# A recurrent layer whose convolution stays in fp32, with its products on VectorE and its squares on ScalarE

## The chip, the core and the metric

The kernel runs on one core of one Trainium2 chip. The time is the device time of one execution in microseconds (us), before: 1421.28 us, the median of three runs (1419.26 to 1422.52). The engines are TensorE (PE in the profile; its weight loads are PEld), VectorE (DVE), ScalarE (ACT), GpSimd (POOL) and the queue SyncE (SP), which issues most of the loads.

## The reference

A trunk of two layers over 512 tokens of 1024 features. Each layer is a mixer, a cross-attention into 256 memory tokens and a SwiGLU FFN, each with a norm in front and a residual add behind. Layer 1's mixer is the recurrent block on which the change works:

```
z = h @ w_in                                   # [512, 2048]
gate_branch, xb = split(z, 2)
xb = causal_depthwise_conv(xb, conv_w, conv_b) # width 4
r = sigmoid(xg @ w_rgate + b_r); i = sigmoid(xg @ w_igate + b_i)   # 4 heads of 256
log_a = -8 * r * softplus(-lam)
a = exp(log_a); mult = sqrt(-expm1(2 * log_a)) # a = 0 and mult = 1 where positions == 0
b = mult * (i * xb)
hseq = scan: h[t] = a[t] * h[t-1] + b[t]
y = (gelu(gate_branch) * hseq) @ w_out
```

The cross-attention of a layer norms the memory, with a gain of that layer, and makes keys and values of it: `m = rms_norm(mem, norm_mem[layer]); k, v = split(m @ w_kv, 2)`.

## The kernel before

Activations lie with features on the partitions, as tiles of 128 features by 512 tokens. Every product of TensorE is made of three: weights and activations are each split into a high part (float32r) and a low part (what is left), and `mm3` sums high by high, high by low and low by high (lines 166, 167 and 168). One output tile of 128 features from 1024 is 24 matmuls of 512 columns.

**Weights.** `Weights.get` loads 512 KB over SP into one of two raw buffers (tag `wraw`), casts it on ScalarE to the high part (line 98) and subtracts on VectorE for the low part (line 99); there are three buffers for each part. So VectorE has one subtraction of 1024 columns for each output tile.

**Banks.** `linear` writes to a PSUM bank with the tag `mm` or `att`; there are two of each. A third tile on `mm` needs the first one read out.

**The recurrent block (`odd`).** `conv_tile(m)` makes one tile of xb, multiplies it by the norm's row (826), runs the four taps on VectorE (829, 831) into a temporary `t0`, and splits that into high and low for the gate products (153, 154). `lru_gates` makes the tiles `r` and `i` of a head (sigmoids, 841); then GpSimd adds the high and low part of the convolution to get it back (879) and multiplies `i` by it (880), VectorE scales `r` (881), and ScalarE writes tanh into a tile `h` (841). `gate_tile(m)` makes a tile of the gate branch and VectorE reads it out of `mm` (904, tile `g`). `lru_scan` runs exp on all eight `r`, squares them on GpSimd (890, into `t0`, of which there are two), combines on VectorE (891), runs sqrt on ScalarE, multiplies (895) and scans (896) on VectorE. ScalarE needs one table for exp, another for sqrt and another for GeLU, and `run()` keeps each kind together. Then GpSimd multiplies GeLU of the gate by the scan (918), the result is split (153, 154) and goes into `out_proj`.

**The memory.** `mem_gained(layer, ...)` loads the memory, multiplies it by its norm's row on GpSimd (348) and splits it with the layer's gain on ScalarE and VectorE (156, 157) into the tile `mg`. `odd` calls it for layer 1 and makes the keys (`mem_keys`, weights `xk`, copies out of `mm` at 362); `cross(1)` calls it once more for the values.

**Order.** A scheduler works out the order of each engine from a timeline of its own when the program is built. What it may move it moves, over the borders of the stages too. `tc.issue_after` holds some instructions behind others.

Of the kernel before, what the change touches and what calls it, by code (L numbers as in the profile page):

```python
# [9 lines left out]
F32 = mybir.dt.float32  # L10
# [3 lines left out]
AF = mybir.ActivationFunctionType  # L14
ALU = mybir.AluOpType
AX = mybir.AxisListType
PSUM = bass.MemoryType.PSUM

P = 128
T = 512  # L20
D = 1024
KD = D // P
# [46 lines left out]
class Weights:  # L69
    """Streams [n, 128, F] blocks and splits each into float32r high and low parts."""  # L70
# [33 lines left out]
class Trunk:  # L104
# [23 lines left out]
    def pair(self, side, n=T):  # L128
        """High and low parts of an activation tile, from one of the two sides of the activation store."""
        return tuple(self.actp.tile([P, n], F32R, name=self.nm(f"act{side}"), tag=f"act{side}") for _ in range(2))  # L130
# [7 lines left out]
    def bank(self, tag="mm"):  # L138
        """A PSUM bank: mm and att for products, s for scores, tr for transposes and row sums."""
        if tag == "any":  # L140
            self.flip ^= 1
            tag = ("mm", "att")[self.flip]
        return self.psum.tile([P, T], F32, name=self.nm(tag), tag=tag, bufs=BANKS[tag])
# [15 lines left out]
    def mm3(self, out, terms, begin=True, end=True):  # L159
        """out = sum over terms of (wh + wl).T @ (xh + xl), less wl.T @ xl.  # L160

        A sum in pieces has its first one with begin and its last one with end."""
        nc = self.nc
        last = len(terms) - 1
        for i, (wh, wl, xh, xl) in enumerate(terms):
            nc.tensor.matmul(out, wh, xh, start=begin and i == 0, stop=False)  # L166
            nc.tensor.matmul(out, wh, xl, start=False, stop=False)  # L167
            self.mm_ins = nc.tensor.matmul(out, wl, xh, start=False, stop=end and i == last).ins  # L168

    def rstd_cols(self, *sums, inner=None, bank="tr"):  # L170
        """For each (ssq, dim, tiles, scale): [128, tiles] columns of scale * rsqrt(column sums of ssq / dim + eps).

        With inner the squared values are still to be scaled by these columns, and so is what the result scales."""
        nc = self.nc
        ps = self.bank(bank)
        n = sum(s[2] for s in sums)
        v = self.small(8)
        o = 0
        for ssq, dim, nt, _ in sums:
            terms = ssq if isinstance(ssq, tuple) else (ssq,)  # L180
            for t in range(nt):
                for i, a in enumerate(terms):
                    self.sum_ins = nc.tensor.matmul(ps[:, o + t:o + t + 1], a[:, t * P:(t + 1) * P], self.ones[:, 0:1],  # L183
                                                    start=i == 0, stop=i == len(terms) - 1).ins
            o += nt
        o = 0
        if inner is not None:
            sq = self.small(8)
            nc.vector.tensor_mul(sq[:, :inner.shape[-1]], inner, inner)
        for _, dim, nt, _ in sums:  # L190
            if inner is None:
                nc.vector.tensor_scalar(v[:, o:o + nt], ps[:, o:o + nt], 1.0 / dim, EPS, op0=ALU.mult, op1=ALU.add)
            else:
                nc.vector.scalar_tensor_tensor(v[:, o:o + nt], ps[:, o:o + nt], 1.0 / dim, sq[:, :nt],
                                               op0=ALU.mult, op1=ALU.mult)
            o += nt
        if inner is not None:
            nc.vector.tensor_scalar(v[:, :n], v[:, :n], EPS, None, op0=ALU.add)
        r = self.rsqrt(v, n)
        res, o = [], 0  # L200
        for _, _, nt, scale in sums:
            if inner is not None:
                nc.vector.scalar_tensor_tensor(r[:, o:o + nt], r[:, o:o + nt], scale or 1.0, inner,
                                               op0=ALU.mult, op1=ALU.mult)
            elif scale is not None:
                nc.vector.tensor_scalar(r[:, o:o + nt], r[:, o:o + nt], scale, None, op0=ALU.mult)
            res.append(r[:, o:o + nt])
            o += nt
        return res

    def rsqrt(self, v, n):
        """v ** -0.5 of n columns, refined by one step."""
        nc = self.nc
        y, w, r = (self.small(8)[:, :n] for _ in range(3))
        v = v[:, :n]
        nc.gpsimd.tensor_tensor(y, v, self.mhalf[:, :n], op=ALU.pow)
        nc.vector.tensor_mul(w, y, y)
        nc.vector.tensor_mul(w, w, v)
        nc.vector.tensor_scalar(w, w, -0.5, 1.5, op0=ALU.mult, op1=ALU.add)
        nc.vector.tensor_mul(r, y, w)  # L220
        return r

    def bcast(self, cols, nt=NT, bank="tr"):
        """PSUM tile [128, nt*128] with the columns' values along the free axis, on every partition."""
# [27 lines left out]
    def next_norm(self, side, gain, off):  # L252
        """State for the norm that follows a residual update: filled tile by tile."""
        return {"side": side, "gain": gain, "off": off, "ssq": self.new_ssq(), "xg": []}
# [9 lines left out]
    def linear(self, W, blk, xs, off=0, bank="mm", ps=None, k0=0, k1=None):  # L264
        """One output tile: block blk of W holds its k tiles side by side. With k0 and k1 a piece of the sum."""
# [18 lines left out]
    def setup(self):  # L284
# [6 lines left out]
        # the table of the first functions is loaded before there is data  # L291
        nc.scalar.activation(self.small(1), self.ones[:, 0:1], AF.Square)
        # the array's clock is raised while the first operands are on their way
# [29 lines left out]
    def mem_load(self, keys):  # L323
        """The memory, feature tiles of [128, 256], in the place of the keys to come or among the inputs."""
# [9 lines left out]
    def mem_gained(self, layer, pool, tag, keys=True):  # L334
        """The memory's norm with the layer's gain, split: feature tiles [128, 256], high and low."""
# [17 lines left out]
    def mem_keys(self, layer, mg, m0, m1, low=None):  # L353
        """Keys of the memory, [features, memory tokens]."""
# [9 lines left out]
    def rope_table(self, pool, C):  # L364
        """C: rows 0:64 one, 64:96 cos, 96:128 sin with the sign of its half.

        Worked out with 16 frequencies x 8 chunks of the positions on the partitions."""
# [49 lines left out]
    def even(self, nrm, nxt_spec):  # L417
# [4 lines left out]
        with ExitStack() as ctx:  # L422
# [10 lines left out]
            # latents: z[0:2] of the queries, z[2] of keys and values, z[3] rotary keys and their swapped halves  # L433
# [36 lines left out]
            # queries and keys of two pairs of heads; rows 64:128 of the keys stay  # L470
# [10 lines left out]
            # pooling mixer  # L481
# [31 lines left out]
            # latent attention  # L513
# [22 lines left out]
            def v_pair(wh, wl):  # L536
                """Values of two heads, tokens on partitions."""
# [99 lines left out]
    def cross(self, layer, nrm, nxt_spec, mg=None):  # L637
# [3 lines left out]
        with ExitStack() as ctx:  # L641
# [40 lines left out]
            def scores(hd):  # L682
                """Softmax of one head's scores, queries on partitions, two query tiles side by side."""
# [63 lines left out]
    def ffn(self, layer, nrm, nxt_spec):  # L747
# [12 lines left out]
        for pi, nf in enumerate(FFN_PARTS):  # L760
# [3 lines left out]
            for f in range(f0, f0 + nf):  # L764
                pg = self.linear(Wg, (layer * NF + f) * 2, xg, bank="mm")
                pu = self.linear(Wg, (layer * NF + f) * 2 + 1, xg, bank="att")
                if R is None:
                    R = self.norm_row(nrm["ssq"], D)
                t = self.tmp("t0")
# [17 lines left out]
    def odd(self, nrm, nxt_spec):  # L787
# [6 lines left out]
        with ExitStack() as ctx:  # L794
# [6 lines left out]
            # 8 * softplus(-lambda) = 8 * (max(-lambda, 0) + log1p(exp(-|lambda|)))  # L801
# [20 lines left out]
            def conv_tile(m, bank="mm"):  # L822
# [4 lines left out]
                t = self.tmp("t0")  # L827
# [11 lines left out]
            def act(out, src, fn, **kw):  # L839
                """A function of ScalarE's tables; run() keeps those of a kind together."""  # L840
                table.append(nc.scalar.activation(out, src, fn, **kw).ins)
# [12 lines left out]
            def lru_gates():  # L854
                for hd in range(4):
                    if hd == 0:
                        # the row of the norm's factors comes between the first tiles
# [10 lines left out]
                    for d in range(2):  # L868
# [8 lines left out]
                        xh, xl = xc[m]  # L877
                        x = self.tmp("t1")
                        nc.gpsimd.tensor_add(x, xh[:, :].bitcast(F32), xl[:, :].bitcast(F32))
                        nc.gpsimd.tensor_mul(is_[m], is_[m], x)  # L880
                        nc.vector.scalar_tensor_tensor(rs[m], rs[m], c8[:, m:m + 1], rst, op0=ALU.mult, op1=ALU.add)
                        ts[m] = pool.tile([P, T], F32, name=f"h{m}", tag=f"h{m}")
                        act(ts[m], rs[m], AF.Tanh)

            def lru_scan():
                with run():
                    for m in ms:
                        a2 = self.tmp("t0")
                        act(rs[m], rs[m], AF.Exp, scale=-1.0)
                        nc.gpsimd.tensor_mul(a2, rs[m], rs[m])  # L890
# [19 lines left out]
            mg = self.mem_gained(1, pool, "mg")  # L910
            gates = [gate_tile(m) for m in range(KD)]
            self.mem_keys(1, mg, 0, KD, None)
# [4 lines left out]
            for m, t in enumerate(gates):  # L917
                nc.gpsimd.tensor_mul(hs[m], t, hs[m])
# [7 lines left out]
    def tail(self, W, ys, base, side):  # L926
        """The last projection, its residual and the final norm: features on partitions for the first tokens,
        tokens on partitions for the last ones."""
# [38 lines left out]
        def after(n):  # L967
            """The sums and the row of the norm come in between these products."""
# [31 lines left out]
def tile_trunk(ctx: ExitStack, tc: tile.TileContext, ins, out):  # L1000
    k = Trunk(ctx, tc, ins, out)
    nrm = k.setup()
    stages = [
        lambda n: k.even(n, ("xa_norm_x", 0)),
        lambda n: k.cross(0, n, ("ffn_norm", 0)),
        lambda n: k.ffn(0, n, ("od_norm", 0)),
        lambda n: k.odd(n, ("xa_norm_x", KD)),
        lambda n: k.cross(1, n, ("ffn_norm", KD)),
        lambda n: k.ffn(1, n, None),
    ]  # L1010
    for s in stages:
        nrm = s(nrm)
# [78 lines left out]
```

## Time and profile before

| | |
|---|---|
| span of the profiled execution | 1418.8 us |
| its own time | the profile gives the span alone |
| median of the runs | 1421.28 us (1419.26 to 1422.52) |
| instructions | 16758 |
| busy PE, DVE, ACT, POOL | 1384.2, 784.9, 549.6, 321.7 us |
| mean granted TensorE clock | 0.989 of full speed |
| the recurrent block | about 710 to 912 us of the span |

Busy times are sums of instructions of an engine over the span. Where a matmul follows another, the profile counts TensorE as busy throughout, so a share near 100% is the most that can be read there. A wait is named after the engine whose work ended it.

### The profile page before, as it was taken

How to read it: one execution, taken by the hardware profiler on the slowest of the kernel's cores; microseconds unless marked ns; L12 is line 12 of the kernel's file. 1: busy time of each engine (PE TensorE's matmuls, PEld its weight loads, DVE VectorE, ACT ScalarE, POOL GpSimd, SP SyncE). 2: the span in 40 equal slices, each digit the busy share in tenths (PEclk: the TensorE clock that was granted, in tenths of full speed). 3: DMA queues.
4: the chain of work that ended last, by engine and by line, in shares of the span. 5: the costliest groups of instructions: out<-in, count | busy, mean ns of one | idle time of the engine just before them, and what ended most of it. 6: DMA issues, size and time to landing. Idle time of an engine off the chain costs nothing.

```text
span 1418.8 us, 16758 instructions
## 1 busy us (share of the span) xinstructions
PE 1384.2 (98%) x6524; PEld 1153.3 (81%) x6524; DVE 784.9 (55%) x1043; ACT 549.6 (39%) x859; POOL 321.7 (23%) x291
## 2 busy tenths in 40 slices
PE   8989999999999999999999989999999999999997
PEld 6878888878888888888887778888888888888887
DVE  7687574456454345344579796445545534453553
ACT  6466553454332232223434555335433312221331
POOL 4586261103110011001234470211121100110112
PEclk8999999999999999999999989999999999999999
DMA  6222162323223233332322334322323333323331
GB/s 208 75 71 79 60 193 79 115 60 118 90 90 104 89 104 92 102 90 93 108 89 90 98 105 154 96 71 91 116 89 93 100 96 98 99 84 111 93 104 60
DMA packets 45326, 140.28 MB, mean 99 GB/s; under 512 B 5568, under 2 KB 10816, under 8 KB 45248
## 3 DMA queue, kind: packets, MB, share of 16 engines
q1 hardware_dynamic: 43808, 137.91, 31.1%
q10 hardware_dynamic: 1440, 1.32, 0.3%
q8 instruction: 51, 0.84, 0.2%
q14 instruction: 27, 0.22, 0.0%
HBM read 136.98 MB, written 2.10 MB: 98 GB/s over the span
## 4 chain that ended last, share of the span: by engine, by line
PE 86%; DVE 7%; issue 2%; ACT 2%; DMA 1%; POOL 1%; POOLq 0%; SPq 0%; ACTq 0%; DVEq 0%
PE mm L166 16%; PE mm L168 16%; PE mm L167 16%; PE att L166 10%; PE att L168 10%; PE att L167 10%; DMA dn_raw<-in_ffn_down_dram 1%; DVE h L896 1%; DVE act L154 1%; PE s L166 1%; PE s L167 1%; PE s L168 1%; DVE i L895 1%; PE tr L183 1%; PE mm L667 1%
## 5 line engine op out<-in xcount | busy, mean ns | idle before, releaser
L98 ACT CAST gu_h<-gu_raw 128x1024 fp32r<-128x1024 f32 x88 | 92.8, 1054 | 293.0 <-PE mm L167 162.7
L774 POOL TENSOR_TENSOR t<-t,t 128x512 f32<-128x512 f32 x44 | 60.0, 1364 | 577.9 <-ACT gu_h L98 383.1
L99 DVE TENSOR_TENSOR gu_l<-gu_raw,gu_h 128x1024 fp32r<-128x1024 f32 x88 | 138.2, 1570 | 33.1 <-ACT gu_h L98 33.1
L166 PE MATMUL att<-act,gu_h 128*128 128x512 f32 x352 | 137.8, 391 | 0.0
L166 PE MATMUL mm<-act,gu_h 128*128 128x512 f32 x352 | 137.1, 390 | 0.0
L168 PE MATMUL att<-act,gu_l 128*128 128x512 f32 x352 | 137.0, 389 | 0.0
L167 PE MATMUL mm<-act,gu_h 128*128 128x512 f32 x352 | 136.9, 389 | 0.0
L168 PE MATMUL mm<-act,gu_l 128*128 128x512 f32 x352 | 136.9, 389 | 0.0
L167 PE MATMUL att<-act,gu_h 128*128 128x512 f32 x352 | 136.9, 389 | 0.0
L247 POOL TENSOR_TENSOR ssq<-ssq,t 128x512 f32<-128x512 f32 (+1 forms) x49 | 77.5, 1582 | 196.5 <-ACT t L246 188.5
L773 DVE TENSOR_TENSOR t<-att,R 128x512 f32<-128x512 f32 x44 | 30.4, 691 | 128.3 <-PE att L168 128.3
L98 ACT CAST dn_h<-dn_raw 128x1024 fp32r<-128x1024 f32 (+1 forms) x40 | 40.3, 1011 | 138.2 <-PE att L167 102.5
L167 PEld LDWEIGHTS att<-act,gu_h 128*128 128x128 f32 x352 | 66.2, 188 | 14.2 <-issue 0.5
L166 PEld LDWEIGHTS att<-act,gu_h 128*128 128x128 f32 x352 | 66.0, 188 | 14.1 <-issue 0.5
L168 PEld LDWEIGHTS mm<-act,gu_l 128*128 128x128 f32 x352 | 66.1, 188 | 13.9
L168 PEld LDWEIGHTS att<-act,gu_l 128*128 128x128 f32 x352 | 66.0, 188 | 13.7
L167 PEld LDWEIGHTS mm<-act,gu_h 128*128 128x128 f32 x352 | 66.0, 187 | 13.7
L166 PEld LDWEIGHTS mm<-act,gu_h 128*128 128x128 f32 x352 | 66.1, 188 | 13.5
L274 DVE TENSOR_TENSOR x<-mm,x 128x512 f32<-128x512 f32 x44 | 30.3, 690 | 83.4 <-PE mm L168 82.6
L770 DVE TENSOR_TENSOR t<-mm,R 128x512 f32<-128x512 f32 x44 | 30.4, 691 | 69.6 <-PE mm L168 66.8
L153 ACT CAST act<-t 128x512 fp32r<-128x512 f32 (+1 forms) x53 | 32.9, 621 | 71.9 <-POOL t L774 56.0
L99 DVE TENSOR_TENSOR dn_l<-dn_raw,dn_h 128x1024 fp32r<-128x1024 f32 (+1 forms) x40 | 56.2, 1408 | 6.6 <-ACT dn_h L98 6.6
(397 smaller groups left out, 3541.8 us busy)
## 6 DMA issues: line engine op xcount, KB each, us to landing
gu_raw<-in_ffn_gu_dram SPq DMA_DIRECT2D x88, 512.0 KB, 3.5
dn_raw<-in_ffn_down_dram SPq DMA_DIRECT2D x32, 512.0 KB, 3.6
xk_raw<-in_xa_w_k_dram SPq DMA_DIRECT2D x16, 512.0 KB, 3.5
xq_raw<-in_xa_w_q_dram SPq DMA_DIRECT2D x16, 512.0 KB, 3.6
xv_raw<-in_xa_w_v_dram SPq DMA_DIRECT2D x16, 512.0 KB, 3.5
xo_raw<-in_xa_w_o_dram SPq DMA_DIRECT2D x16, 512.0 KB, 3.6
odin_raw<-in_od_w_in_dram SPq DMA_DIRECT2D x16, 512.0 KB, 3.5
dn_raw<-in_ffn_down_dram SPq DMA_DIRECT2D x16, 384.0 KB, 3.0
```

The source lines that it names most:

```text
L98: nc.scalar.copy(hi, src)
L99: self.low.tensor_sub(lo, src, hi[:, :].bitcast(F32))
L153: nc.scalar.copy(hi, src)
L154: nc.vector.tensor_sub(lo, src, hi.bitcast(F32))
L166: nc.tensor.matmul(out, wh, xh, start=begin and i == 0, stop=False)
L167: nc.tensor.matmul(out, wh, xl, start=False, stop=False)
L168: self.mm_ins = nc.tensor.matmul(out, wl, xh, start=False, stop=end and i == last).ins
L247: nc.gpsimd.tensor_add(ssq[:, :n], ssq[:, :n], sq[:, :n])
L274: self.nc.vector.tensor_add(self.x[m], ps, self.x[m] if src is None else src)
L770: nc.vector.tensor_mul(t, pg, R)
L773: nc.vector.tensor_mul(u, pu, R)
L774: nc.gpsimd.tensor_mul(u, u, t)
```

## The change

Five edits:

- The convolution's result goes into the tile `h` of the block's pool and stays there in fp32; GpSimd's sum of the two parts (879) is dropped.
- The product of `i` and the convolution (880) and that of GeLU and the scan (918) are on VectorE.
- The squares (890) are on ScalarE.
- `mem_gained` for layer 1 is called within the first FFN, after its fifth tile, and its tile lies in a pool of its own.
- `cross(1)` takes that tile, so that the second load, scaling and split of the memory are gone.

```
-                t = self.tmp("t0")
+                t = ts[m] = pool.tile([P, T], F32, name=f"h{m}", tag=f"h{m}")
...
-                        xh, xl = xc[m]
-                        x = self.tmp("t1")
-                        nc.gpsimd.tensor_add(x, xh[:, :].bitcast(F32), xl[:, :].bitcast(F32))
-                        nc.gpsimd.tensor_mul(is_[m], is_[m], x)
+                        nc.vector.tensor_mul(is_[m], is_[m], ts[m])
                         nc.vector.scalar_tensor_tensor(rs[m], rs[m], c8[:, m:m + 1], rst, op0=ALU.mult, op1=ALU.add)
-                        ts[m] = pool.tile([P, T], F32, name=f"h{m}", tag=f"h{m}")
                         act(ts[m], rs[m], AF.Tanh)
...
                         act(rs[m], rs[m], AF.Exp, scale=-1.0)
-                        nc.gpsimd.tensor_mul(a2, rs[m], rs[m])
+                        nc.scalar.activation(a2, rs[m], AF.Square)
                         nc.vector.scalar_tensor_tensor(ts[m], a2, 1.0, ts[m], op0=ALU.add, op1=ALU.mult)
...
-            mg = self.mem_gained(1, pool, "mg")
             gates = [gate_tile(m) for m in range(KD)]
-            self.mem_keys(1, mg, 0, KD, None)
+            self.mem_keys(1, self.mg, 0, KD, None)
...
-                nc.gpsimd.tensor_mul(hs[m], t, hs[m])
+                nc.vector.tensor_mul(hs[m], t, hs[m])
...
+                if aside and f == 4:
+                    aside()
...
+    with tc.tile_pool(name="mg1", bufs=1) as pool:
+        def ready():
+            k.mg = k.mem_gained(1, pool, "mg")
+
+        nrm = k.ffn(0, nrm, ("od_norm", 0), ready)
+        nrm = k.odd(nrm, ("xa_norm_x", KD))
+        nrm = k.cross(1, nrm, ("ffn_norm", KD), k.mg)
```

What it does to the order is seen at three places. The first is VectorE near the end of the first cross-attention, ahead of the first FFN: `mg` is layer 1's split memory and `x` a residual. Before:

```order
L157 SCALAR_TENSOR_TENSOR mg_6544<-keys_6539,vecs,mg_6544 128x256 x5
L274 TENSOR_TENSOR x<-mm_3229,x 128x512
L157 SCALAR_TENSOR_TENSOR mg_6544<-keys_6539,vecs,mg_6544 128x256
L274 TENSOR_TENSOR x<-mm_3266,x 128x512
L157 SCALAR_TENSOR_TENSOR mg_6544<-keys_6539,vecs,mg_6544 128x256 x2
```

Now:

```order
L157 SCALAR_TENSOR_TENSOR mg_3916<-keys_3911,vecs,mg_3916 128x256 x5
L274 TENSOR_TENSOR x<-mm_3229,x 128x512
L157 SCALAR_TENSOR_TENSOR mg_3916<-keys_3911,vecs,mg_3916 128x256 x2
L274 TENSOR_TENSOR x<-mm_3266,x 128x512
L157 SCALAR_TENSOR_TENSOR mg_3916<-keys_3911,vecs,mg_3916 128x256
```

The split stands at the same place in both, ahead of the FFN; one of its eight instructions has changed sides with a residual.

The second place is VectorE in the middle of the scans, up to the last read-out of the gate tiles (`g`), with line 896 (now 894) the scans and `xk_l` and `odin_l` the low parts of weights. Before:

```order
L904 TENSOR_TENSOR g_6765<-mm_6740,R_5977 128x512
L99 TENSOR_TENSOR xk_l_6836<-xk_raw_6833,xk_h_6835 128x1024
L895 TENSOR_TENSOR i_6507<-h_6513,i_6507 128x512
L896 SCALAR_TENSOR_TENSOR h_6397<-r_6382,i_6391 128x512
L895 TENSOR_TENSOR i_6531<-h_6537,i_6531 128x512
L904 TENSOR_TENSOR g_6798<-mm_6773,R_5977 128x512
```

Now:

```order
L902 TENSOR_TENSOR g_6744<-mm_6719,R_6010 128x512
L99 TENSOR_TENSOR xk_l_6815<-xk_raw_6812,xk_h_6814 128x1024
L894 SCALAR_TENSOR_TENSOR h_6314<-r_6379,i_6388 128x512
L893 TENSOR_TENSOR i_6522<-h_6448,i_6522 128x512
L894 SCALAR_TENSOR_TENSOR h_6357<-r_6400,i_6409 128x512
L893 TENSOR_TENSOR i_6543<-h_6491,i_6543 128x512
L915 TENSOR_TENSOR h_6046<-g_6579,h_6046 128x512
L915 TENSOR_TENSOR h_6089<-g_6612,h_6089 128x512
L915 TENSOR_TENSOR h_6132<-g_6645,h_6132 128x512
L915 TENSOR_TENSOR h_6175<-g_6678,h_6175 128x512
L902 TENSOR_TENSOR g_6777<-mm_6752,R_6010 128x512
```

Four products of line 915 now stand between the sixth and the seventh read-out, and two more between the seventh and the eighth (not shown); the last two follow behind it.

The third place is ScalarE behind the last tanh, where the exps end (the last `r`) and the sqrts begin (`h<-h`). Before:

```order
L841 ACTIVATE r_6498<-r_6498 128x512
L841 ACTIVATE r_6522<-r_6522 128x512
L98 CAST odin_h_6736<-odin_raw_6734 128x1024
L841 ACT_TABLE_LOAD
L841 ACTIVATE h_6179<-h_6179 128x512
```

Now:

```order
L843 ACTIVATE r_6513<-r_6513 128x512
L843 ACTIVATE r_6534<-r_6534 128x512
L888 ACTIVATE t_929_7068<-r_6197 128x512
L888 ACTIVATE t_930_7072<-r_6218 128x512
L98 CAST odin_h_6715<-odin_raw_6713 128x1024
L888 ACTIVATE t_931_7076<-r_6245 128x512
L843 ACT_TABLE_LOAD
L843 ACTIVATE h_6046<-h_6046 128x512
```

The squares (888) follow all eight exps, and from the fourth on they alternate with the sqrts; the program holds ten table loads in both versions. On TensorE the order is the same up to the gate products and again from the keys on; between, the last matmul of the gate products stands 17 matmuls further ahead.

## Rows read from the trace of the kernel before

**Rows 1.** Stretches A:B in us: length, then busy time by engine, granted clock, DMA.

```profile
745.00:850.00 105.00, 94.75 (x440) 78.28 (x439) 92.64 (x88) 54.19 (x80) 58.50 (x40) 0.95 0.33 96
850.00:915.00 65.00, 63.36 (x327) 54.28 (x326) 34.17 (x48) 32.01 (x53) 12.31 (x7) 1.00 0.41 129
```

**Rows 2.** The same view, finer, where VectorE is busy throughout.

```profile
810.00:820.00 10.00, 3.89 (x15) 2.95 (x14) 10.00 (x10) 3.03 (x4) 7.91 (x7) 0.90 0.46 134
820.00:830.00 10.00, 10.00 (x35) 8.00 (x35) 10.00 (x10) 4.59 (x8) 7.04 (x5) 0.76 0.45 131
830.00:850.00 20.00, 16.54 (x115) 15.69 (x114) 20.00 (x16) 10.71 (x19) 14.87 (x8) 0.91 0.28 82
```

**Rows 3.** TensorE in order of time: start, us, instruction; in brackets the wait.

```profile
812.03 0.39 PE L167 MATMUL mm<-act,odin_h 128*128 128x512 f32 x1
812.26 0.39 PE L168 MATMUL mm<-act,odin_l 128*128 128x512 f32 x1
818.76 0.76 PE L166 MATMUL mm<-act,odin_h 128*128 128x512 f32 x1 [6.11 <-DVE g L904]
...
838.86 0.55 PE L166 MATMUL mm<-mg,xk_h 128*128 128x256 f32 x1 [3.27 <-DVE g L904]
...
862.76 0.40 PE L166 MATMUL mm<-act,odout_h 128*128 128x512 f32 x1
```

**Rows 4.** TensorE's waits from 740 to 860 us: total, times, longest.

```profile
PE mm L166 <- ACT keys L362: 1.6, 1, 1.6
```

**Rows 5.** VectorE, 798 to 851 us, groups: total, mean ns, idle time before.

```profile
L896 DVE TENSOR_TENSOR_SCAN h<-r,i 128x512 f32<-128x512 f32 x8 | 12.8, 1605 | 0.0
L895 DVE TENSOR_TENSOR i<-h,i 128x512 f32<-128x512 f32 x8 | 9.6, 1205 | 0.0
L154 DVE TENSOR_TENSOR act<-h,act 128x512 fp32r<-128x512 f32 x8 | 8.3, 1090 | 0.0
L99 DVE TENSOR_TENSOR xk_l<-xk_raw,xk_h 128x1024 fp32r<-128x1024 f32 x5 | 7.5, 1506 | 0.0
L891 DVE SCALAR_TENSOR_TENSOR h<-t,h 128x512 f32<-128x512 f32 x8 | 7.5, 942 | 2.6 <-POOL t L890 2.6
L99 DVE TENSOR_TENSOR odin_l<-odin_raw,odin_h 128x1024 fp32r<-128x1024 f32 x3 | 5.0, 1651 | 0.0
```

**Rows 6.** The same view from 850 to 912 us.

```profile
L99 DVE TENSOR_TENSOR xk_l<-xk_raw,xk_h 128x1024 fp32r<-128x1024 f32 x3 | 3.7, 1225 | 3.9 <-ACT xk_h L98 3.9
...
L154 DVE TENSOR_TENSOR act<-h,act 128x512 fp32r<-128x512 f32 x2 | 1.3, 678 | 0.0
```

**Rows 7.** VectorE in order of time, within the scans.

```profile
798.43 2.11 DVE L891 SCALAR_TENSOR_TENSOR h<-t,h 128x512 f32<-128x512 f32 x2 [1.62 <-POOL t L890]
...
812.09 0.68 DVE L895 TENSOR_TENSOR i<-h,i 128x512 f32<-128x512 f32 x1
812.69 1.21 DVE L896 TENSOR_TENSOR_SCAN h<-r,i 128x512 f32<-128x512 f32 x1
...
835.89 2.22 DVE L99 TENSOR_TENSOR xk_l<-xk_raw,xk_h 128x1024 fp32r<-128x1024 f32 x1
838.03 0.68 DVE L904 TENSOR_TENSOR g<-mm,R 128x512 f32<-128x512 f32 x1
```

**Rows 8.** GpSimd, all its groups from 798 to 851 us.

```profile
L918 POOL TENSOR_TENSOR h<-g,h 128x512 f32<-128x512 f32 x8 | 16.1, 2044 | 0.0
L890 POOL TENSOR_TENSOR t<-r 128x512 f32<-128x512 f32 x8 | 11.1, 1400 | 5.3 <-DVE h L891 4.6 <-ACT r L841 0.7
L348 POOL TENSOR_TENSOR mem<-mem,Rmem 128x256 f32<-128x256 f32 x8 | 10.8, 1380 | 5.1 <-DVE g L904 3.0 <-DMA mem<-in_memT_dram 2.1
```

**Rows 9.** ScalarE in order of time, at the end of the gates.

```profile
794.71 0.62 ACT L841 ACTIVATE h<-r 128x512 f32<-128x512 f32 x1
...
796.65 4.28 ACT L841 ACTIVATE r<-r 128x512 f32<-128x512 f32 x8
```

**Rows 10.** The chain that ended last, near the first cross-attention's end: start, us.

```profile
314.33 1.98 DVE mg L157 x5
```

More of the change, by code (lines that the diff above doesn't have):

```diff
@@ L745, in cross, with ffn @@
         return nxt
-    def ffn(self, layer, nrm, nxt_spec):
+    def ffn(self, layer, nrm, nxt_spec, aside=None):
         nc, ins = self.nc, self.ins
@@ L1002, in tile_trunk @@
     nrm = k.setup()
[L1003 to L1012, printed above, removed]
+    nrm = k.even(nrm, ("xa_norm_x", 0))
+    nrm = k.cross(0, nrm, ("ffn_norm", 0))
+    with tc.tile_pool(name="mg1", bufs=1) as pool:
[4 more added lines that the diff above has]
+        nrm = k.cross(1, nrm, ("ffn_norm", KD), k.mg)
+    k.ffn(1, nrm, None)
 def layout(inputs):
```

## Prediction

> **What bounds the kernel now.** I read the busy time by stretches first. TensorE is busy 1384.2 of 1418.8 us, so nothing is to be had where it runs without a gap, and every stage that the change touches has to be looked at for gaps of TensorE alone. There is one large hole: from 745 to 850 us, the recurrent block, TensorE is busy 94.75 of 105 us at a granted clock of 0.95, and 63.36 of 65 in the next 65 us [rows 1]. Cut finer, the hole is where the scans are: VectorE is busy in every microsecond from 810 to 850, TensorE 3.89 of 10 us at first, and the clock goes down to 0.76 behind that gap and is 0.91 after it [rows 2]. That is 0.76 of the higher level (2.4 GHz) as a mean over the stretch, so part of it ran at the lower one (1.2 GHz).
>
> Then TensorE in order of time, to see who ends its waits. The two long ones, 6.11 and 3.27 us, are both ended by `g`, VectorE's read-out of a gate tile from an `mm` bank [rows 3]. There are two such banks, and TensorE can't begin the third tile on before VectorE has read out the first. The read-outs aren't slow (0.68 us); they stand in VectorE's queue behind the scans, products and weight subtractions. So the end of the stage is set by VectorE's queue up to the eighth read-out, at 838.03 us [rows 7]. From there TensorE makes the memory's keys, and the output projection begins at 862.76 us, 23.9 us after the keys resume at 838.86 [rows 3].
>
> Why is VectorE's queue that long? The same instructions take very different times. A scan takes 1.61 us in the mean of eight but 1.21 in one case, a product (895) 1.21 against 0.68 [rows 5, 7]; subtractions of weights take 1.65 and 1.51, but 1.23 from 850 on, and the subtraction of 512 columns 1.09 against 0.68 [rows 5, 6]. GpSimd is what differs: it works 38.0 us in the slow stretch (16.1, 11.1 and 10.8) [rows 8] and 12.31 of 65 from 850 on [rows 1]; the two fast instructions at 812 us fall where it waited 2.1 us for a DMA [rows 7, 8]. Read-outs from PSUM keep their 0.68 us even while GpSimd works [rows 7]. ScalarE and the DMA are no less busy from 850 to 915 than before [rows 1], so they don't explain it.
>
> **The change, part by part.** Up to the scans' last read-out, by VectorE's queue:
>
> *Slowing that goes.* All GpSimd work named in rows 8 is gone: the products go to VectorE, the squares to ScalarE, and the memory's eight scalings (348) aren't done at all. Scans: 8 x (1.605 - 1.21) = 3.2 us. Products 895: 8 x (1.205 - 0.68) = 4.2. Line 891, taken by the same 0.68: 8 x 0.262 = 2.1. The three `odin_l`: 3 x (1.651 - 1.225) = 1.3. Of the `xk_l` one slow one stands ahead of the last read-out: 2.22 - 1.22 = 1.0. Sum 11.8 us off [rows 5 to 7]. The bounds are 0 (the slowing has another cause) and 11.8; I take 11.8, since the fast and the slow instructions part cleanly by whether GpSimd runs.
>
> *Products that come.* The order shows six of the eight new products (915) ahead of the last read-out. They have the form of line 895: 6 x 0.68 = 4.1 us on [rows 7]. Were they still slowed, 6 x 1.205 = 7.2 [rows 5].
>
> *Waits in the queue.* The 2.6 us for GpSimd's squares go [rows 5]. In their place VectorE waits for ScalarE, where a table load and the first sqrt stand between the third square and the first product: I take about 1.0 us, so 1.6 off. Bounds: 0 and, if VectorE waits for one ScalarE instruction at each of the eight tiles, 8 x 0.62 = 5.0 [rows 9].
>
> *Where the queue begins.* It begins at 798.43 us, 1.8 us behind the first exp at 796.65 [rows 7, 9]. Squares now follow all eight exps, so it begins 4.28 + 0.62 = 4.9 us behind: 3.1 us later. But the last gate product stands 17 matmuls further ahead, and a matmul takes 0.23 us (812.03 to 812.26) [rows 3], so the exps begin 3.9 us earlier: 0.8 us off together.
>
> *Behind the last read-out.* The keys' 23.9 us I leave as they are. They hold a wait of 1.6 us for a copy of the keys on ScalarE [rows 4], and half-clock matmuls behind the 3.27 us gap; both may go or stay.
>
> Costed at nothing: the eight products of `i` (880 before) come to VectorE ahead of 795 us, 8 x 0.68 = 5.4 us, and GpSimd's sums (879) and products leave. VectorE had the slowing there too, and TensorE has other tiles to run, so this is covered. If it isn't, it is the new wait of the change: tanh overwrites the convolution, so it must wait for that product. Behind it on ScalarE stand the sigmoids that free the `att` banks, and TensorE's gate products wait for these: at worst 5.4 us. The squares are 8 x 0.62 = 5.0 us on ScalarE, which is busy 54.19 of 105 us [rows 1]. The split of layer 1's memory in the first FFN: five of its eight subtractions ran at 314.33 us already, inside the first cross-attention [rows 10], and the order puts them at the same place now, so that edit does nothing. The memory's second load, its four DMAs on SP and its splits on ScalarE and VectorE go; the splits lay behind 862 us, where TensorE has next to no gap, so only GpSimd's part of that (348) counts, and it is in the sum.
>
> Sum: -11.8 + 4.1 - 1.6 - 0.8 = -10.1 us on the eighth read-out, and as everything behind it is bound by TensorE, on the end: 1418.8 to 1408.7 us in the profile's span. The median of the runs is 2.5 us above that span; I carry the difference over: 1421.3 - 10.1 = 1411.2 us.
>
> One rule speaks against the change. Rows 5 to 8 say that 38.0 us of GpSimd slowed VectorE by some 15 us over the whole stretch (the 11.8, and 3.3 in the subtractions behind the read-out), 0.40 us for each: squares 4.4, memory 4.3, products 6.4 against the 5.4 that eight of them now take. The Trainium skill (Perfetto Trace Analysis, Optimizing Scalar/DVE Operations) holds that the two engines share an SBUF read port, so that moving operations from one to the other might not help; by that alone the move is worth nothing. No run here shows the port itself.
>
> **The rivals.**
>
> *A, the whole hole closes.* VectorE comes free early enough that TensorE never waits. Idle time 10.25 + 1.64 = 11.9 us [rows 1], lost clock 0.24 x 10 + 0.09 x 20 = 4.2 [rows 2]: 16.1 us off, 1405.2 us. Against it: up to the eighth read-out VectorE still has the scans and six more products.
>
> *B, ScalarE and VectorE wait for each other.* Squares need one of two `t0` buffers, which VectorE must read first; sqrts alternate with them; tanh waits for the product. At 5.0 us, as above, -5.1 is left: 1416.2 us. For it: the alternation in the order. Against: ScalarE's idle half.
>
> *C, moving products gives nothing.* What the six products take equals what they had cost, and the squares and the scalings had only slowed VectorE where TensorE was covered (ahead of 812 us it had no long wait). Left are the 1.0 us between 6.4 and 5.4: 1420.3 us, no change. The rule above is this case. Against: GpSimd's scalings fall between 813 and 829 us, in the hole.
>
> *D, slower.* VectorE's long instructions have another cause than GpSimd, and stay long. Then the six products cost 7.2 us, the other two terms give back 2.4: 4.8 us more, 1426.1 us. It decides from the point at which less than 4.1 - 2.4 = 1.7 of the 11.8 us go. Against: rows 6, with ScalarE and DMA as busy.
>
> **How the numbers follow.** Forecast (1408.5 to 1414.5) 0.55; A (below 1408.5) 0.13; B (1414.5 to 1418.4) 0.21; C 0.06; D 0.05. Faster or slower means by over 0.2% (2.8 us), about what a measurement of this kernel can tell from no change: faster 0.55 + 0.13 + 0.21 = 0.89, same 0.06, slower 0.05. The range 1406 to 1418 us takes in the forecast, nearly all of B and over half of A, 0.83 together.
>
> **What would show it.** Scans at 1.21 us, products 893 and 915 at 0.68 and GpSimd idle through the stretch show the first two terms; if scans stay near 1.6, D. The eighth read-out some 10 us earlier, near 828 us, and a gap of TensorE ahead of it that is shorter than 3 us show the sum; many short waits of VectorE for ScalarE's sqrts and squares show B. A loss of TensorE ahead of 795 us shows that tanh's new wait isn't covered. The FFNs and the tail should be as before.

## The result, and the profile after

The changed kernel takes 1409.4 us (median of four runs, 1408.22 to 1410.8), the kernel before beside it on the same chip 1420.27 us: a ratio on record of 0.9916, 95% interval 0.9904 to 0.9928 (the two medians alone give 0.9923). The forecast was 1411.2 us, with a range from 1406 to 1418. The profiled execution took 1408.22 us, with a span of 1406.4 us.

Stretches of the span (length; busy time of PE, PEld, DVE, ACT and POOL with their instructions; granted clock; DMA), the ones of [rows 1, 2]:

```profile
745.00:850.00 105.00, 99.52 (x511) 84.77 (x510) 83.57 (x112) 64.49 (x100) 0.20 (x2) 0.98 0.34 105
850.00:915.00 65.00, 65.00 (x309) 54.72 (x308) 29.47 (x40) 24.98 (x34) 13.57 (x8) 1.00 0.35 116
810.00:820.00 10.00, 9.36 (x41) 7.39 (x41) 10.00 (x13) 6.32 (x11) 0.00 (x0) 1.00 0.33 103
820.00:830.00 10.00, 7.68 (x56) 6.85 (x54) 10.00 (x14) 6.21 (x11) 0.00 (x0) 1.00 0.17 56
830.00:850.00 20.00, 17.92 (x136) 17.64 (x135) 14.97 (x22) 11.89 (x22) 0.00 (x0) 0.91 0.50 153
```

The hole has shrunk: TensorE is idle 5.48 of 105 us where it was idle 10.25. It now does 9.36 of 10 us in the stretch where it did 3.89. GpSimd does nothing at all between 810 and 850 us, and VectorE has room again behind 830. The answers to [rows 3, 4], TensorE in order of time with its waits:

```profile
809.74 0.47 PE L166 MATMUL mm<-act,odin_h 128*128 128x512 f32 x1 [0.19 <-DVE g L902]
816.11 0.47 PE L166 MATMUL mm<-act,odin_h 128*128 128x512 f32 x1 [0.65 <-DVE g L902]
823.69 0.36 PE L166 MATMUL mm<-mg,xk_h 128*128 128x256 f32 x1 [1.86 <-DVE g L902]
827.26 0.39 PE L166 MATMUL mm<-mg,xk_h 128*128 128x256 f32 x1 [0.46 <-ACT keys L362]
835.71 0.39 PE L166 MATMUL mm<-mg,xk_h 128*128 128x256 f32 x1 [2.08 <-ACT keys L362]
...
851.47 0.39 PE L166 MATMUL mm<-act,odout_h 128*128 128x512 f32 x1
```

The waits of 6.11 and 3.27 us for a read-out of `g` are now 0.65 and 1.86, and one of 2.08 for a copy of the keys follows. The answers to [rows 5], VectorE's groups from 790 to 845 us (total, mean ns, idle time before):

```profile
L894 DVE TENSOR_TENSOR_SCAN h<-r,i 128x512 f32<-128x512 f32 x8 | 9.8, 1219 | 0.0
...
L893 DVE TENSOR_TENSOR i<-h,i 128x512 f32<-128x512 f32 x8 | 5.5, 682 | 0.6 <-ACT h L843 0.6
L889 DVE SCALAR_TENSOR_TENSOR h<-t,h 128x512 f32<-128x512 f32 x8 | 5.4, 681 | 2.8 <-ACT t L888 2.8
L915 DVE TENSOR_TENSOR h<-g,h 128x512 f32<-128x512 f32 x8 | 5.2, 684 | 0.0
L154 DVE TENSOR_TENSOR act<-h,act 128x512 fp32r<-128x512 f32 x8 | 5.2, 688 | 0.0
```

Every group runs at its short duration: scans at 1.22 us, products and splits at 0.68. The answers to [rows 7], VectorE in order of time where its queue begins, among the new products and at the last read-out:

```profile
796.79 1.29 DVE L889 SCALAR_TENSOR_TENSOR h<-t,h 128x512 f32<-128x512 f32 x2 [2.83 <-ACT t L888]
...
820.45 2.49 DVE L915 TENSOR_TENSOR h<-g,h 128x512 f32<-128x512 f32 x4
822.86 0.69 DVE L902 TENSOR_TENSOR g<-mm,R 128x512 f32<-128x512 f32 x1
...
828.04 0.67 DVE L902 TENSOR_TENSOR g<-mm,R 128x512 f32<-128x512 f32 x1
```

To compare profiles I measure the stage by itself, since executions reach it up to 3 us apart with the same code ahead of it. It opens with the column sums of the recurrent norm and closes with those of the next norm (line 183, eight matmuls each; the last one's start counts). Of the kernel before, then of the changed one (minimum, median and maximum ns, first and last start):

```profile
L183 PE MATMUL tr<-ones,ssq x8: 165/250/250, 716.0 to 716.7; 128*128 128x1 f32 x8
L183 PE MATMUL tr<-ones,ssq x8: 165/250/250, 914.2 to 914.9; 128*128 128x1 f32 x8
```

```profile
L183 PE MATMUL tr<-ones,ssq x8: 166/250/251, 714.5 to 715.2; 128*128 128x1 f32 x8
L183 PE MATMUL tr<-ones,ssq x8: 166/250/251, 902.9 to 903.6; 128*128 128x1 f32 x8
```

The stage took 914.9 - 716.7 = 198.2 us before and takes 903.6 - 715.2 = 188.4 now: 9.8 us less. The other 2.6 of the 12.4 us between the two spans lie outside of it: 1.5 ahead of its opening, 1.1 behind its close. They belong to the single execution: a second profile of the changed kernel has a stage of 187.5 us and a span of 1410.9.

### The profile page after: what moved, and what is told of

It is laid out like the page before. It is cut to its first block, busy times and chain, and to the rows that moved or that the text cites. A ratio compares the mean times of both kernels' runs of the same rounds, so it can differ in the third digit from the quotient of the medians.

```text
span 1406.4 us, 16696 instructions
## 1 busy us (share of the span) xinstructions
PE 1377.7 (98%) x6524; PEld 1149.8 (82%) x6524; DVE 766.1 (54%) x1051; ACT 551.3 (39%) x859; POOL 256.3 (18%) x251
## 4 chain that ended last, share of the span: by engine, by line
PE 88%; DVE 6%; ACT 2%; issue 2%; DMA 1%; POOL 0%; POOLq 0%; ACTq 0%; DVEq 0%
PE mm L166 17%; PE mm L168 17%; PE mm L167 17%; PE att L167 10%; PE att L168 10%; PE att L166 10%; DMA dn_raw<-in_ffn_down_dram 1%; PE s L166 1%; PE s L167 1%; PE s L168 1%; PE tr L183 1%; PE att L666 1%; PE mm L667 1%; PE att L667 1%; PE mm L666 1%
## 5 line engine op out<-in xcount | busy, mean ns | idle before, releaser
L247 POOL TENSOR_TENSOR ssq<-ssq,t 128x512 f32<-128x512 f32 (+1 forms) x49 | 76.8, 1568 | 269.4 <-ACT t L246 261.5
L167 PEld LDWEIGHTS mm<-act,gu_h 128*128 128x128 f32 x352 | 66.1, 188 | 13.7
L168 PE MATMUL mm<-act,dn_l 128*128 128x512 f32 x152 | 59.2, 390 | 0.0
```

The source lines that it names most:

```text
L247: nc.gpsimd.tensor_add(ssq[:, :n], ssq[:, :n], sq[:, :n])
```

## The experiments

The experiments were timed in five rounds each, beside the kernel before on the same chip. "Stage" is the length just defined, "read-out" the time from its opening to the eighth read-out of `g`, and DVE and POOL are busy time within the stage, all from one profile.

| run | median us | ratio to before, 95% interval | stage | read-out | DVE | POOL |
|---|---|---|---|---|---|---|
| before | 1421.28 | | 198.2 | 121.3 | 150.9 | 79.0 |
| changed | 1409.40 | 0.9916 (0.9904 to 0.9928) | 188.4 | 112.8 | 132.0 | 15.3 |
| changed, again | 1411.85 | 0.9920 (0.9906 to 0.9934) | 187.5 | 113.0 | 131.8 | 15.2 |
| gate products on GpSimd | 1411.35 | 0.9930 (0.9916 to 0.9943) | 190.6 | 115.1 | 134.6 | 31.1 |
| squares on GpSimd | 1411.57 | 0.9927 (0.9915 to 0.9940) | 188.2 | 114.7 | 136.8 | 26.0 |
| products of `i` on GpSimd | 1411.20 | 0.9930 (0.9918 to 0.9943) | 189.3 | 114.9 | 132.0 | 28.8 |
| memory twice | 1414.24 | 0.9948 (0.9935 to 0.9960) | 192.0 | 117.0 | 138.8 | 26.0 |
| idle multiplies | 1424.18 | 1.0018 (1.0009 to 1.0027) | 201.9 | 127.6 | 147.3 | 50.3 |
| idle copies | 1415.47 | 0.9953 (0.9939 to 0.9966) | 192.9 | 118.4 | 138.0 | 39.2 |
| split in the layer | 1410.28 | 0.9921 (0.9907 to 0.9935) | 188.8 | 113.0 | 132.0 | 15.3 |
| four banks | 1409.14 | 0.9910 (0.9897 to 0.9924) | 187.6 | 112.9 | 132.1 | 15.3 |
| before, four banks | 1421.43 | 0.9999 (0.9990 to 1.0009) | 199.9 | 123.0 | 148.4 | 76.7 |
| products last | 1408.26 | 0.9910 (0.9896 to 0.9923) | 187.2 | 108.6 | 131.5 | 15.3 |
| squares behind own exps | 1408.64 | 0.9911 (0.9897 to 0.9924) | 186.7 | 108.1 | 131.4 | 15.3 |

The two profiles of the changed kernel have a stage of 188.4 and 187.5 us, and the run with the split in the layer, which has the same order on TensorE and GpSimd, 188.8. Differences below are from the mean of the two, 187.95; one under 1.3 us says nothing, and each run has one profile only.

The theory: GpSimd's work stretches what VectorE does beside it, and the stage waits for VectorE. The rivals: GpSimd's late results were the loss (waits); PSUM banks were; moving work between these two engines gives nothing.

**Work on GpSimd that nobody waits for.** This parts the theory from the rival of waits. Behind each exp of the changed kernel stand three more GpSimd instructions:

```
+                idle = self.tmp("t1")
...
                         act(rs[m], rs[m], AF.Exp, scale=-1.0)
+                        for _ in range(3):
+                            nc.gpsimd.tensor_mul(idle, rs[m], rs[m])
```

> The changed kernel with three GpSimd multiplies per feature tile added behind its exp (24, each a row of 512 multiplied by itself into a scratch tile that nobody reads); no other engine's order is changed and nothing is left out. The forecast's theory (GpSimd's work stretches VectorE's instructions beside it, 0.40 us for each us of GpSimd): some 33 us of GpSimd, at the 1.40 us that a square took there before, stretch VectorE by about 13 us, the last gate read-out comes about 10 us later and so does the end, 1417 to 1421. Rival (the gain came from shorter chains of waits, since GpSimd's results came late): nobody waits for these multiplies, so no change from 1409.4.

Measured: 1424.18 us, 0.18% slower than the kernel before; the whole gain is gone. The read-out is 14.7 us later and the stage 13.95 us longer. GpSimd runs them without a gap from 795.17 to 831.97 us (start, us):

```profile
795.17 36.80 POOL L892 TENSOR_TENSOR t<-r 128x512 f32<-128x512 f32 x24 [31.74 <-ACT r L843]
```

VectorE in order of time, in the same profile, about the end of that stretch (the new lines shift the numbers by up to three: 896 is the changed kernel's 893, 897 its 894, 905 its 902):

```profile
820.85 0.68 DVE L905 TENSOR_TENSOR g<-mm,R 128x512 f32<-128x512 f32 x1
821.45 1.45 DVE L897 TENSOR_TENSOR_SCAN h<-r,i 128x512 f32<-128x512 f32 x1
...
826.19 1.52 DVE L896 TENSOR_TENSOR i<-h,i 128x512 f32<-128x512 f32 x1
827.64 2.06 DVE L897 TENSOR_TENSOR_SCAN h<-r,i 128x512 f32<-128x512 f32 x1
...
831.00 1.52 DVE L896 TENSOR_TENSOR i<-h,i 128x512 f32<-128x512 f32 x1
...
834.18 1.21 DVE L897 TENSOR_TENSOR_SCAN h<-r,i 128x512 f32<-128x512 f32 x1
835.31 0.66 DVE L896 TENSOR_TENSOR i<-h,i 128x512 f32<-128x512 f32 x1
```

Up to GpSimd's last instruction a scan takes 2.06 us and a product 1.52 (less only right behind a read-out, as at 821.45); with the next one it is 1.21 and 0.66. So GpSimd's presence alone stretches VectorE, by 15.4 us for 35.0 us (the rows' sum of the 24): 0.44 for each. The rival of waits falls: no wait in this stretch ends at one of these multiplies. VectorE's delay reaches TensorE over ScalarE too: TensorE's longest wait there, 8.8 us, is for ScalarE's cast of the first weights of the keys, which stands behind sqrts that waited 4.7 and 4.2 us for VectorE.

**The same with copies.** The edit is `nc.gpsimd.tensor_copy(idle, rs[m])` in the place of the multiply.

> As the run with the idle multiplies, but each is a copy, which reads one operand; nothing is left out. If GpSimd's work stretches VectorE by being there, as the forecast has it, the loss is again 0.40 us for each us of GpSimd. If it is the operands that GpSimd reads that count, the copies cost half of that or nothing. Rival of waits: no change.

Measured: 1415.47 us, the stage 4.95 us longer, the read-out 5.5 us later. GpSimd's group from 740 to 860 us (total, mean ns), and VectorE in order of time beside it:

```profile
L892 POOL COPY t<-r 128x512 f32<-128x512 f32 x24 | 23.9, 997 | 33.2 <-ACT r L843 31.7
```

```profile
801.90 1.09 DVE L896 TENSOR_TENSOR i<-h,i 128x512 f32<-128x512 f32 x1
802.92 0.68 DVE L905 TENSOR_TENSOR g<-mm,R 128x512 f32<-128x512 f32 x1
...
805.13 1.62 DVE L897 TENSOR_TENSOR_SCAN h<-r,i 128x512 f32<-128x512 f32 x1
```

A product is 1.09 us instead of 0.68, a scan 1.62 instead of 1.21: 0.41 longer each, where beside multiplies it was 0.85. VectorE lost 6.1 us for 23.9 us of GpSimd, 0.26 for each. So a flat 0.40 for each us is wrong. The copies cost about half of what the multiplies did, which the expectation's second branch had for the operands that GpSimd reads. But a copy is also shorter than a multiply (last section), and this run doesn't tell operands from length.

**The gate products back on GpSimd.** Line 915 with `nc.gpsimd`.

> The eight products of the gates with the scan's results go back to GpSimd; nothing is left out. The forecast's theory (GpSimd's work stretches the VectorE instructions that run beside it): six products leave the queue ahead of the last gate read-out, 4.1 us less, and the 16.1 us of GpSimd, at 0.40 us of VectorE each, give 6.4 back, less what falls behind that read-out. So 0 to 3 us more than the changed kernel's 1409.4, scans again over 1.3 us, and the last gate read-out 0 to 3 us later. Rival (GpSimd costs VectorE nothing, the products only lengthened VectorE's queue): 4.1 us less, near 1405.

Measured: the stage is 2.65 us longer and the read-out 2.2 us later; the ratio points the same way, but its interval overlaps with that of the changed kernel. The rival's 4.1 us of gain isn't there. Two groups of VectorE's (790 to 845 us), beside 15.9 us of GpSimd:

```profile
L894 DVE TENSOR_TENSOR_SCAN h<-r,i 128x512 f32<-128x512 f32 x8 | 12.4, 1547 | 0.0
...
L893 DVE TENSOR_TENSOR i<-h,i 128x512 f32<-128x512 f32 x8 | 7.5, 941 | 0.6 <-ACT h L843 0.6
```

VectorE has eight products fewer (4.8 us, at 0.60 from start to start) and is still busy 2.7 us longer: the products cost it about 7.5 us from GpSimd.

**The squares back on GpSimd.** Line 888 with `nc.gpsimd.tensor_mul(a2, rs[m], rs[m])`.

> The eight squares go back to GpSimd; nothing is left out. The forecast's theory: 11.1 us of GpSimd stretch VectorE by 4.4 us, and the wait for GpSimd's squares (2.6) takes the place of that for ScalarE's (1.0): about 6 us more, near 1415. Rival (no stretching, the waits alone): 1.6 us more, near 1411.

Measured: no difference, the stage 0.25 us longer, where 6 were expected. The stretching is there: VectorE is busy 4.9 us longer for 10.7 us of GpSimd. But its queue begins earlier, as GpSimd squares while ScalarE still runs the exps:

```profile
795.70 1.51 DVE L889 SCALAR_TENSOR_TENSOR h<-t,h 128x512 f32<-128x512 f32 x1 [2.63 <-POOL t L888]
```

That is 795.70 - 717.1 = 78.6 us behind the opening, against 796.79 - 715.2 = 81.6: 3.0 us earlier. The read-out is 1.8 us later, about the 4.9 less these 3.0, but that doesn't reach the end of the stage. My expectation had left out this term, which the prediction has (3.1).

**The products of `i` back on GpSimd.** Line 879 with `nc.gpsimd`, on the fp32 convolution.

> The eight products of the input gates with the conv output go back to GpSimd, on the fp32 conv output that is kept; nothing is left out. The forecast's theory: these products lie in a stretch where TensorE has its own work and VectorE has room, so their 5.4 us on VectorE were free: within 1.5 us of 1409.4. Rival (VectorE's queue is one chain from the conv tiles on): 5 us less, near 1404.

Measured: the stage is 1.35 us longer and the read-out 2.0 later, at the edge of what can be told. VectorE is busy equally long, 132.0 us: what eight products take is what they cost it from GpSimd. What moves is the last tanh, which waits for the product (ScalarE in order of time):

```profile
795.93 0.64 ACT L843 ACTIVATE h<-r 128x512 f32<-128x512 f32 x1 [1.85 <-POOL i L879]
...
797.88 1.68 ACT L843 ACTIVATE r<-r 128x512 f32<-128x512 f32 x3
```

The exps begin 797.88 - 718.3 = 79.6 us behind the opening; with the products on VectorE it is 791.96 - 715.2 = 76.8.

**The memory loaded, scaled and split twice.** `cross(1)` is called without the kept split.

> Layer 1's cross attention loads, scales and splits the memory again, as before the change, and the kept split serves the keys alone; nothing is left out. The forecast's theory: this work has cover behind the output projection of the recurrent layer and counts only for what GpSimd takes from VectorE there, where no TensorE work waits for VectorE: within 1.5 us of 1409.4. Rival (its 10.8 us of GpSimd count wherever they lie, at 0.40): 4.3 us more, near 1414.

Measured: 1414.24 us, the stage 4.05 us longer and the read-out 4.1 later. Of these four runs it is the one whose ratio is clear of both of the changed kernel's. The figure is the rival's; its reason, that this work counts wherever it lies, isn't shown, since I had the place wrong. The scheduler doesn't leave this work behind the output projection: GpSimd does it in the middle of the scans (in order of time):

```profile
808.74 2.25 POOL L348 TENSOR_TENSOR mem<-mem,Rmem 128x256 f32<-128x256 f32 x2 [46.27 <-DMA mem<-in_memT_dram]
...
821.29 2.65 POOL L348 TENSOR_TENSOR mem<-mem,Rmem 128x256 f32<-128x256 f32 x2 [2.46 <-DMA mem<-in_memT_dram]
```

**The split in the recurrent layer.** `mem_gained(1, ...)` stands in `odd` again and its tile is kept for `cross(1)`.

> Layer 1's memory is again scaled and split at the place in the code where it was, in the recurrent layer, and still kept for the cross attention; nothing is left out. The forecast's theory: the scheduler puts this work at the head of the stage either way, so no change from the 1409.5 to 1411 of the changed kernel. Rival (the split in the FFN frees VectorE and GpSimd in the recurrent layer): 0.40 of its 10.8 us of GpSimd come back, 4.3 us more.

Measured: no difference (0.9921, the stage 188.8). Where the call stands in the code does nothing; that the tile is kept does.

**Four banks for the gate products.** Line 900 becomes `self.linear(Win, m, xg, bank="any")`, in the changed kernel and, in another run, in the kernel before.

> The changed kernel with the eight gate products going to four banks of PSUM in turn, not two; nothing is left out. The forecast's theory (in this stage TensorE waits for the gate read-outs in VectorE's queue): the 2.7 us of waits for read-outs go, and as the last read-out is no earlier, the keys' first products may wait in their place; 0 to 3 us less, 1406.5 to 1409.4. Rival (VectorE's queue alone sets when the keys can be finished): no change.

> The kernel before with the gate products on four banks of PSUM; nothing is left out. The forecast's theory: VectorE's queue, stretched by GpSimd, is the limit, and four banks only let TensorE run ahead of it: 0 to 4 us less than before, ratio 0.997 to 1.000. Rival (TensorE's 9.4 us of waits for the read-outs are a matter of banks): 9 us less, ratio near 0.993, all that the change brought.

Measured: no difference in either. In the kernel before, none of the 9.4 us of waits for `g` is left, yet nothing is won, as TensorE now waits for the next thing in the same queue, the low parts of weights:

```profile
PE mm L168 <- DVE odin_l L99: 3.6, 2, 2.8
PE mm L168 <- DVE xk_l L99: 2.7, 1, 2.7
PE att L168 <- DVE odin_l L99: 2.5, 1, 2.5
```

The rival of banks falls: they only chose which of VectorE's results TensorE waits for.

**The products behind the last read-out, and the squares meant to stand between the exps.** The first run is the changed kernel with four banks and each product of line 915 under `tc.issue_after` of the eighth read-out; the second also has

```
-                        a2 = self.tmp("t0")
+                        a2 = self.tmp(("t0", "t1")[m % 2])
                         act(rs[m], rs[m], AF.Exp, scale=-1.0)
-                        nc.scalar.activation(a2, rs[m], AF.Square)
+                        with tc.issue_after(table[-1]):
+                            table.append(nc.scalar.activation(a2, rs[m], AF.Square).ins)
```

> The changed kernel with the gate products on four banks and the eight products of the gates with the scan's results held back until the last gate read-out; nothing is left out. The forecast's theory puts a price of 4.1 us on the six products ahead of that read-out: it comes 4 us earlier, some 109 us behind the stage's row sums, and the time falls by 0 to 4 us, as the weights' splits of the keys may bind next. Rival (the queue as a whole must be done, in whatever order): read-out earlier, time the same.

> As the run with the products last, and each square on ScalarE straight behind its exp, not all squares behind all exps; nothing is left out. The forecast's theory put 3.1 us on the squares' late start: VectorE's 2.8 us of idle time ahead of the first product with a square goes, the last gate read-out comes 2 to 3 us earlier still, near 106 us, and the time falls by 0 to 3 us more. Rival (as above): the time stays.

Measured: the read-out comes 4.3 us earlier in the first, 4.8 in the second, where 2 to 3 more were expected from the squares. The second edit didn't do what it was meant to: it holds each square behind its own exp, but no exp behind a square. ScalarE still runs eight exps first, and VectorE waits 2.77 us for the first square (in order of time):

```profile
790.51 4.28 ACT L843 ACTIVATE r<-r 128x512 f32<-128x512 f32 x8
794.70 1.14 ACT L889 ACTIVATE t<-r 128x512 f32<-128x512 f32 x2
795.35 1.29 DVE L890 SCALAR_TENSOR_TENSOR h<-t,h 128x512 f32<-128x512 f32 x2 [2.77 <-ACT t L889]
```

So what earlier squares would be worth is untested. The stage is shorter by 0.75 and by 1.25 us, and the ratios, 0.9910 and 0.9911, lie within the interval of the changed kernel. Both beat the kernel before, but that they beat the changed kernel is not shown. TensorE's waits from 735 to 860 us in the first (total, times, longest):

```profile
PE mm L166 <- ACT keys L362: 3.5, 3, 2.0
PE att L166 <- ACT r L843: 1.3, 2, 0.7
```

No wait for `g` is left; the copies of the keys on ScalarE are next. The theory's 4.1 us for the six products was right for the read-out, and of little worth for the end, as the rival had it. The rival's reason, that the whole queue must be done, isn't shown: from 784 to 830 us of the first run TensorE is busy 46.00 of 46 us, so it waits for nothing of VectorE's there.

## Why the prediction was right, and where its terms were off

The cause was right: GpSimd's 38.0 us beside the scans were what made VectorE long, shown by work that has no other effect (idle multiplies). The time was 1.8 us under the forecast. One reading was loose: ScalarE is a little less busy behind 850 us than ahead of it (0.49 of the time against 0.52, [rows 1]); the idle multiplies, which give ScalarE nothing to do, settle that rival. Against the stage, the terms are these:

- *Slowing that goes, -11.8*: the same groups give 11.7 (scans 3.1, products 893 4.2, line 889 2.1, `odin_l` 1.3, `xk_l` 1.0). Right.
- *Products that come, +4.1*: they stand 0.60 us apart, since the profile's 0.68 overlaps the next instruction's start: 6 x 0.60 = 3.6. Four of them with their overlap are the 2.49 us at 820.45.
- *Waits, -1.6*: the step that failed. Of the 2.6 us that I let go, 1.62 lie ahead of 798.43 [rows 7], where the term "where the queue begins" starts; I counted them twice. Inside the queue the kernel before waits 0.94 us and the changed one 0.82: -0.1.
- *Where the queue begins, -0.8*: measured from the opening, at 798.43 - 716.7 = 81.7 before and 81.6 now: -0.1. The exps begin 3.2 us earlier, not 3.9, and the squares' late start takes that back.
- *The read-out*: -11.7 + 3.6 - 0.1 - 0.1 = -8.3, measured 112.8 - 121.3 = -8.5, forecast -10.1.
- *Behind it, left as it is*: also off. From the eighth read-out to the output projection it took 862.76 - 838.03 = 24.7 us and takes 851.47 - 828.04 = 23.4. The prediction names 3.3 us of stretching in the subtractions there and gives their going no value. They are at 0.69 now, but they aren't where the 1.3 us come from: before, TensorE waited 0.20 us in all for a subtraction there.

So -8.5 and -1.3 make the stage's -9.8, and that the forecast of -10.1 came close is luck: two errors of some 1.5 us cancel.

The sum that holds goes by TensorE's own waits. Before, TensorE resumed the keys when the eighth read-out was done, at 838.86, with 24 of their 192 matmuls done. Now it starts the keys when the seventh is done (it begins at 822.86, TensorE's wait ends at 823.69), and no wait of TensorE ends at the eighth. From there to the output projection, before with its wait for a subtraction, then now (the first busy time is PE's):

```profile
838.86:862.76 23.90, 22.06 (x168) 21.65 (x169) 16.74 (x15) 13.13 (x22) 6.01 (x4) 0.94 0.52 163
846.61 0.39 PE L168 MATMUL mm<-mg,xk_l 128*128 128x256 f32 x1 [0.20 <-DVE xk_l L99]
...
823.69:851.47 27.78, 25.24 (x193) 24.75 (x194) 21.78 (x30) 17.59 (x32) 0.00 (x0) 0.94 0.43 136
```

Behind the opening, that wait ends at 838.86 - 716.7 = 122.2 us before and at 823.69 - 715.2 = 108.5 now: 13.7 earlier. What follows is 3.9 us longer: one tile of the keys more (25.24 - 22.06 = 3.2) and 0.7 more of waits (0.46 and 2.08, where it was 1.64 and 0.20). Together -9.8.

So the step from the eighth read-out to the end had the wrong marker. What follows the read-out is bound by TensorE and the copies of the keys in these rows, but in the changed kernel TensorE doesn't wait for that read-out; with the products held back it came 4.3 us earlier and the stage gained 0.75.

*By edit.* Undone one at a time, the stage lengthens by 2.65 us (gate products), 1.35 (products of `i`), 0.25 (squares) and 4.05 (the second memory), 8.3 of about 10.25 together; that these add up isn't shown, and GpSimd's sum (879), which was dropped too, no run puts back. The prediction had 1.0, nothing, some 2.9 (squares: 4.4 + 1.6 less 3.1 for their late start) and 4.3. The memory fits. For the squares it was too high, as the wait of 1.6 wasn't there; and what it costed at nothing, the products of `i`, may have been worth about 1, at the edge of what can be told.

*Rivals.* A (1405.2) isn't reached: TensorE still waits 5.2 us in the rows above. B's waits of VectorE for ScalarE stay at 0.82 us in the queue. D falls with the idle multiplies, C by the result. By VectorE's time, the products of `i` cost it the same from either engine; the gate products cost it about 7.5 from GpSimd and 4.8 on VectorE. C's rule, from the Trainium skill (Perfetto Trace Analysis, Optimizing Scalar/DVE Operations), is that moving work between the two engines might not help. The products of `i` agree with it and the gate products don't, and it can't speak of work that goes to ScalarE or isn't done.

## What to carry to other kernels

When one form of instruction shows two durations in a trace, look at what another engine does in each of them, and test it with work that nobody waits for. An engine that is off every chain of waits can still cost the engine beside it. Where the end of a stage hangs on a queue, look in the rows for the last wait of TensorE that ends in it, before and after: a marker such as the last read-out counts only while such a wait ends there. Count an idle gap in one term only. And when an edit is to change an order, read the order from the trace before reading the time.

## What the runs showed of the hardware that I had not expected

The stretching is not a lower rate but a piece for each instruction, whatever its own length. Beside the idle multiplies a product goes from 0.67 to 1.52 us and a scan, nearly twice as long, from 1.21 to 2.06: 0.85 both. Beside copies it is 0.41 for both. Read-outs from PSUM keep 0.68 us in the midst of it, and the scan right behind the one at 820.85 loses 0.24 only.

GpSimd is held up as well. Its idle multiplies ahead of VectorE's queue and beside it (795 to 799.6 and 799.6 to 833 us), then the idle copies ahead of it (793 to 797.25 us; total, mean ns):

```profile
L892 POOL TENSOR_TENSOR t<-r 128x512 f32<-128x512 f32 x4 | 4.2, 1041 | 32.0 <-ACT r L843 31.7
L892 POOL TENSOR_TENSOR t<-r 128x512 f32<-128x512 f32 x20 | 30.8, 1542 | 1.6
...
L892 POOL COPY t<-r 128x512 f32<-128x512 f32 x7 | 4.3, 618 | 32.1 <-ACT r L843 31.7
```

Undisturbed, a multiply takes 1.04 us and a copy 0.62, and each holds a VectorE instruction up by at most some 0.2 us less than that. The number of operands alone doesn't set it: the memory's scalings read two, of 256 columns, take 0.73 us where they are shortest, and lengthen a scan beside them from 1.21 to 1.76 us (memory twice), 0.55. Which engine starts first matters. In the kernel before, a scan that starts ahead of a square keeps its time and the square is long; the subtraction that starts within the square is long itself:

```profile
809.04 1.21 DVE L896 TENSOR_TENSOR_SCAN h<-r,i 128x512 f32<-128x512 f32 x1
809.26 1.83 POOL L890 TENSOR_TENSOR t<-r 128x512 f32<-128x512 f32 x1 [1.89 <-DVE h L891]
810.17 1.99 DVE L99 TENSOR_TENSOR odin_l<-odin_raw,odin_h 128x1024 fp32r<-128x1024 f32 x1
```

The Trainium skill (SBUF — State Buffer, SBUF: two separate sides) says that GpSimd and a VectorE instruction with two SBUF inputs lock each other out for a whole instruction. The trace agrees with a wait once per instruction, on either side, and with the spared read-outs, which have one input in PSUM. It shows nearly the whole of an undisturbed GpSimd instruction as VectorE's loss, 0.85 of 1.04 us and 0.41 of 0.62; the 1.46 us that a multiply is drawn in the mean (35.0 / 24) have GpSimd's own waiting in them.
